# A two-layer attention trunk: norm weights applied at the evacuation of the turned blocks, value projections token by token

## The chip, the cores and the metric

One NeuronCore of one Trainium2 chip runs the kernel. The metric is the device time of one execution in microseconds (us).

## The reference

Two layers work on x of 512 tokens by 1024 channels: `x <- x + RMSNorm(Mixer(RMSNorm(x, norm_pre[i])), norm_post[i])`. Layer 0 mixes with sparse attention of three branches (compressed, selected, window; 16 heads in 4 groups), layer 1 with differential attention (8 heads). What the change touches is the start of each:

```python
u = rmsnorm(x, norm_pre[i])          # x * rsqrt(mean(x*x) + EPS) * g
q, kc, vc, ks, vs, kw, vw, gate, z = jnp.split(u @ w_in, points, axis=-1)   # layer 0
gate = sigmoid(gate)
q, k, v, z = jnp.split(u @ w_in, 4, axis=-1)                               # layer 1
```

All is float32.

## The kernel before, in words

**Products.** Every operand of a projection is cut in two parts of type float32r: hi, a rounded copy, and lo, the rest. A projection is then three products (hi x hi, lo x hi, hi x lo). Activations are turned so that channels lie on partitions: eight blocks of 128 channels for each of four token tiles of 128 tokens. The turned u is kept as `bigA` (hi) and `bigB` (lo) in layer 0, `bigF` and `bigE` in layer 1; `bigD` and `bigC` hold the normed x before it is turned.

**Norm.** `prenorm` (L355) takes one token tile: two Squares with sums on ScalarE (L361), a few 128x1 instructions on VectorE for the root (L335 to L352), and two 128x512 passes that write x * r * g (L373; g is a row of norm weights spread over all partitions, tiles `P`, loaded at L298 as two transfers of 256 KB). In layer 1 (`early`) GpSimd multiplies with g beforehand (L364) and VectorE scales with two pointer scalars (L369). `turn` transposes four blocks into one PSUM bank `T` (L380), and ScalarE and VectorE evacuate the bank in one instruction each: hi (L100, 128x512) and lo (L105, 128x512).

**Weights.** `Stream` loads weight pieces on the SP queue (L126) and splits them into whi and wlo. Who splits is set by tables: the first letter names the engine of the hi (A ScalarE, P GpSimd), the second that of the lo (D VectorE, P GpSimd). Without an entry GpSimd does both (L165, L167). Each split lets the load of the second next piece follow on the SP queue.

**Start.** The jobs `vs` and `vw` (value projections, 256 and 304 columns; 48 of the 304 are the gate) come first, then the compressed keys and values `kc0, kc1, vc0, vc1` (L198, 24 matmuls of 128x512 each, evacuated by `evac_cmp` with two ScalarE and two VectorE copies, L399 and L400, from the two `mm` banks). The value jobs use L218; `vw` runs cut by cut over all tokens, two tokens in a bank. `turn_small` (L711, L714) comes between kc1 and vc0. The gate's Tanh is taken per token in `evac_v` (L432), and one VectorE instruction scales the gate (L780, 128x192, two immediate numbers). Seven matmuls on zeros (L306) run before the first data.

**Between the layers.** `o1` is the second half of layer 0's output projection (L467). While it ends, VectorE and GpSimd norm the tokens of layer 1. `dv0` and `dv1` are the first value projections there; the order of token tiles is written out in `SEQ` (a and b are steps of dv0 and dv1 with the token's number, p is a `turn`), TensorE keeping exactly that order. dv0 keeps two tokens in each of two `S` banks; ScalarE evacuates it at L571. VectorE makes the lo of dv1's first piece (L160, tile `wx`), GpSimd its hi.

## Time and profile before

| | us |
|---|---|
| median of 3 runs | 666.04 |
| lowest, highest | 665.90, 666.87 |
| profiled execution: its own time | 669.65 |
| profiled execution: span | 667.8 |
| TensorE busy | 638.7 (96%) |
| VectorE busy | 427.7 (64%) |
| GpSimd busy | 401.6 (60%) |
| ScalarE busy | 338.9 (51%) |

The chain of work that ended last is 78% TensorE, 14% VectorE, 3% ScalarE, 2% DMA, 2% issue. The mean granted clock of the profiled execution is 0.986 of full. The span is the stretch from the first to the last instruction of the trace; the execution's own time is 1.85 longer, and the profiled execution took 3.61 longer than the median of the timed runs. In the 40 slices of the page TensorE is at 90% or more nearly everywhere; the first two slices (0 to 33 us) show 6 and 8 tenths.

### The profile page before, as it was taken

The page shows a single profiled execution, that of the slowest core. Times are in us where ns is not written, and L with a number is a line of the kernel's source. Part 1 is how long each engine was busy: PE and PEld are TensorE (multiplying, and loading weights), DVE is VectorE, ACT ScalarE, POOL GpSimd, SP SyncE. Part 2 cuts the span into 40 slices and gives each one's busy share as a digit, 9 for nine tenths or more (in the row PEclk, how much of TensorE's full clock was granted, in tenths as well). Part 3 has the DMA queues.
Part 4 walks back from the last instruction along what each step waited for, and adds up shares of the span by engine and source line. Part 5 has one row for each costly group of instructions (what it writes and reads, how often), then busy time and mean ns, then how long its engine had stood idle before and what let it go on. Part 6 is the DMA issues. An engine that isn't in the chain of part 4 may idle for free.

```text
span 667.8 us, 11248 instructions
## 1 busy us (share of the span) xinstructions
PE 638.7 (96%) x3773; PEld 558.1 (84%) x3773; DVE 427.7 (64%) x1188; ACT 338.9 (51%) x904; POOL 401.6 (60%) x675
## 2 busy tenths in 40 slices
PE   6899999999999999999999899999999998989996
PEld 5897887888788788888887799888988887879785
DVE  4736245678878878969878800146559658777635
ACT  5311134676667567868563311235464564658431
POOL 4766757868677597668586458948565564413200
PEclk8899999999999999999999999999999998989999
DMA  7546333212122111200852222423223131115302
GB/s 250 151 127 140 107 103 94 64 33 64 32 64 62 35 31 51 62 17 34 301 179 95 95 64 67 124 63 111 73 72 105 47 97 41 62 63 191 126 19 107
DMA packets 68989, 60.52 MB, mean 91 GB/s; under 512 B 3628, under 2 KB 60868, under 8 KB 68932
## 3 DMA queue, kind: packets, MB, share of 16 engines
q1 hardware_dynamic: 68212, 57.45, 29.2%
q10 hardware_dynamic: 720, 2.36, 0.9%
q8 instruction: 30, 0.49, 0.3%
q14 instruction: 27, 0.22, 0.1%
HBM read 55.04 MB, written 4.76 MB: 90 GB/s over the span
## 4 chain that ended last, share of the span: by engine, by line
PE 78%; DVE 14%; ACT 3%; issue 2%; DMA 2%; POOL 0%; SPq 0%; DVEq 0%; ACTq 0%; POOLq 0%
PE mm L198 30%; PE mm L218 11%; PE mm L467 6%; PE T L856 5%; PE av L870 5%; PE S L801 4%; PE S L218 4%; PE S L800 4%; PE S L467 3%; PE av L1166 2%; DVE stk L105 2%; DVE gate L780 2%; PE T L721 1%; PE T L1156 1%; DMA wraw<-in_nsa_w_in_dram 1%
## 5 line engine op out<-in xcount | busy, mean ns | idle before, releaser
L167 POOL TENSOR_TENSOR wlo<-wraw,whi 128x256 fp32r<-128x256 f32 (+2 forms) x247 | 184.0, 772 | 26.9 <-ACT whi L163 26.9
L165 POOL TENSOR_SCALAR whi<-wraw 128x256 fp32r<-128x256 f32 (+1 forms) x240 | 96.2, 426 | 112.7 <-PE mm L198 51.9
L794 ACT ACTIVATE P<-P,st 128x512 f32<-128x512 f32 (+3 forms) x192 | 107.5, 560 | 91.8 <-DVE st L792 91.0
L850 POOL TENSOR_SCALAR P<-P,st,gate 128x512 f32<-128x512 f32 (+3 forms) x128 | 80.1, 636 | 27.1 <-DVE st L847 24.1
L792 DVE CUSTOM_DVE_ANT_0 P<-S,BT 128x128 f32<-128x128 f32 (+2 forms) x144 | 59.7, 419 | 31.2 <-PE S L801 29.0
L198 PE MATMUL mm<-bigA,whi 128*128 128x512 f32 x192 | 77.4, 403 | 1.3 <-DVE bigC L400 1.2
L198 PE MATMUL mm<-bigA,wlo 128*128 128x512 f32 x192 | 75.3, 392 | 0.0
L198 PE MATMUL mm<-bigB,whi 128*128 128x512 f32 x192 | 75.3, 392 | 0.0
L105 DVE TENSOR_TENSOR PT<-T,PT 128x512 fp32r<-128x512 f32 x84 | 56.9, 685 | 8.3 <-ACT PT L100 6.4
L870 PE MATMUL av<-PT,bigE 128*128 128x512 f32 x160 | 56.4, 417 | 1.2 <-DVE bigF L878 0.9
L100 ACT ACTIVATE stk<-mm 64x512 fp32r<-64x512 f32 x64 | 37.9, 592 | 33.2 <-PE mm L198 19.0
L218 PE MATMUL mm<-whi,bigF 128*128 128x256 f32 x176 | 51.4, 293 | 1.7 <-DVE stk L105 1.7
L856 PE MATMUL T<-ident,P 128*128 128x128 f32 x320 | 51.8, 272 | 0.0
L198 PE MATMUL mm<-bigF,whi 128*128 128x512 f32 x128 | 51.7, 404 | 0.0
L100 ACT ACTIVATE PT<-T 128x512 fp32r<-128x512 f32 x84 | 48.6, 592 | 6.0 <-PE T L856 3.9
L198 PE MATMUL mm<-bigF,wlo 128*128 128x512 f32 x128 | 51.3, 401 | 0.0
L856 PEld LDWEIGHTS T<-ident,P 128*128 128x128 f32 x320 | 40.9, 140 | 12.3 <-issue 0.4
L198 PE MATMUL mm<-bigE,whi 128*128 128x512 f32 x128 | 51.1, 399 | 0.0
L218 PE MATMUL mm<-whi,bigE 128*128 128x256 f32 x176 | 50.6, 289 | 0.0
L218 PE MATMUL mm<-wlo,bigF 128*128 128x256 f32 x176 | 50.6, 288 | 0.0
L421 DVE SCALAR_TENSOR_TENSOR stk<-mm,stk 64x512 fp32r<-64x512 f32 x32 | 22.1, 690 | 44.2 <-ACT stk L100 43.4
L198 PEld LDWEIGHTS mm<-bigB,whi 128*128 128x128 f32 x192 | 36.1, 188 | 8.2
(288 smaller groups left out, 1663.4 us busy)
## 6 DMA issues: line engine op xcount, KB each, us to landing
wraw<-in_diff_w_in_dram SPq DMA_DIRECT2D x31, 512.0 KB, 4.0
wraw<-in_nsa_w_in_dram SPq DMA_DIRECT2D x26, 512.0 KB, 3.8
BT<-rd SPq DMA_DIRECT2D x32, 128.0 KB, 3.6
wraw<-in_diff_w_out_dram SPq DMA_DIRECT2D x5, 512.0 KB, 4.0
bigF<-in_x_dram SPq DMA_DIRECT2D x4, 512.0 KB, 9.7
wraw<-in_nsa_w_out_dram SPq DMA_DIRECT2D x4, 512.0 KB, 3.5
bigD<-in_x_dram SPq DMA_DIRECT2D x4, 512.0 KB, 4.7
x1d<-bigD ACTq DMA_DIRECT2D x4, 512.0 KB, 5.2
```

Source lines behind the costliest of these rows:

```text
L100: return nc.scalar.activation(dst, src, AF.Copy, scale=scale)
L105: nc.vector.tensor_tensor(dst, src, h.bitcast(F32), op=OP.subtract)
L165: nc.gpsimd.tensor_scalar(h[:, a:b], v, 1.0, 0.0, op0=OP.mult, op1=OP.add)
L167: e.tensor_tensor(l[:, a:b], v, h[:, a:b].bitcast(F32), op=OP.subtract)
L198: T["mm"] = nc.tensor.matmul(p[:, a:b], wt[:, k, :], u[:, k, a:b], start=(k == 0 and j == 0), stop=(k == KD - 1 and j == 2)).ins
L218: nc.tensor.matmul(acc[t], u[:, k0 + k, t * 128:(t + 1) * 128], wt[:, k, :], start=(ci == 0 and k == 0 and j == 0 and t % per == 0), stop= ...
L467: nc.tensor.matmul(p, U[u][:, k, t * 128:(t + 1) * 128], wt[wi], start=start and j == 0, stop=stop and j == 2, skip_group_check=True)
L792: nc.vector.tensor_tensor_reduce(out=o, in0=i0, in1=b, op0=OP.add, op1=OP.min, scale=-1.0, scalar=BIG, accum_out=nm)
L794: nc.scalar.activation(pt[:, :n], pt[:, :n], AF.Exp, bias=nm, scale=-1.0, accum_out=den)
L850: NORM(nc, i, br, qb).tensor_scalar(self.P[i][:, :n], self.P[i][:, :n], st[:, 8 + i:9 + i], gate[:, NT - 1 - qb, c:c + 1], op0=OP.mult, op ...
L856: T["tmark"] = nc.tensor.transpose(p[:, j * 128:(j + 1) * 128], self.P[j][:, kb * 128:(kb + 1) * 128], ident).ins
L870: nc.tensor.matmul(av, T["V"][:, br, kb, g, :], p, start=(br == 0 and kb == 0 and j == 0), stop=(br == 1 and kb == qb and j == 1))
```

## The change

- **Start.** x's first tile comes in two halves; the norm weights come as 8x128 on the ScalarE queue (4 KB), are turned by TensorE into `gT` (one channel per partition) and copied out (L317). The prenorm of layer 0 then only scales (L385, two pointer scalars), and the norm weight enters at the evacuation: eight ScalarE copies with a scale and eight VectorE instructions (L399), each 128x128, for every token tile, in place of two and two of 128x512. Tiles 1 to 3 take one Square of 1024. Twelve warm-up matmuls in place of seven.
- **Value projections.** `vs` and `vw` run token by token in the order of `SEQ0` (s and w with the token's number, a and b six and two of its eight steps, p a `turn`), each token in a bank of its own. Five pieces are split ahead, vw's hi by ScalarE and lo by GpSimd or VectorE; kc0's and kc1's pieces are split when vw is done.
- **Gate.** It is copied per token, and one Tanh follows for all four.
- **Between the layers.** p1 moves from inside o1 to the head of `SEQ`; dv0 takes one bank per token (S, T, S, S); dv1's first piece is split by ScalarE (hi) and GpSimd (lo).

```diff
-WARM = 7
+WARM = 12
-PRE1 = 29
...
-NS = 4
+NS = 5
...
-SPD = ('PD',)*4
-SEQ = 'a0 a1 p2 b0 b1 a2 p3 b2 a3 b3'.split()
+SPD = ('AP',)*4
+SEQ0 = 's0a p1 s0b s1 w0 w1a p2 w1b s2 w2a p3 w2b w3 s3'.split()
+SEQ = 'p1 a0 a1 p2 b0 b1 a2 p3 b2 a3 b3'.split()
-SPX = ('AP',) * 4
-SPN = 2
-SP0 = ('AP',)*4
-SP1 = ('AD','AD','PP','PP')
+SP0 = (('AP', 'AD', 'AP', 'AP'), ('AD', 'AP', 'AD', 'AP'), ('AP', 'AP', 'AD'), ('AP', 'AP', 'AD'), ('AP', 'AD'))
...
-            bs = [bank(b) for b in banks]
-            per = 4 // len(bs)
-            acc = [bs[t // per][:, (t % per) * n:(t % per) * n + n] for t in range(NT)]
+            if by_token:
+                per, acc = 1, [None] * NT
+            else:
+                bs = [bank(b) for b in banks]
+                per = 4 // len(bs)
+                acc = [bs[t // per][:, (t % per) * n:(t % per) * n + n] for t in range(NT)]
...
             if by_token:
                 for ci in range(len(cuts)):
                     cut[ci] = ws.cut.pop(i + ci)
                 for t in range(NT):
+                    acc[t] = bank(banks[t * len(banks) // NT])[:, :n]
                     for ci in range(len(cuts)):
                         yield from part(ci, t)
                     evac(t, acc[t])
-                for _ in cuts:
-                    if i:
-                        ws.split()
+                for _ in range(len(cuts) if nsplit is None else nsplit):
+                    ws.split()
...
-    load_x(0)
-    gpre = [ptile() for _ in range(2)]
     for i in range(2):
-        nc.sync.dma_start(gpre[i], drows(npre, i * 512, [[0, 128], [1, 512]]))
+        nc.sync.dma_start(xt[:, 0, i * 512:i * 512 + 512], drows(x, i * 512, [[D, 128], [1, 512]]))
+    g8 = work.tile([8, 128], F32, name="g8", tag="P", bufs=NP)
+    gload = nc.scalar.dma_start(g8, drows(npre, 0, [[128, 8], [1, 128]])).ins
...
+    with tc.manual_schedule(engines={mybir.EngineType.PE}):
+        warm(WARM - 7)
+        p = bank("T")
+        nc.tensor.transpose(p[:, 0:8], g8, ident[0:8, 0:8])
+        warm(7)
+    T0["g"] = nc.vector.tensor_copy(gT, p[:, 0:8]).ins
...
+        whole = t and not early
         ss = [small(1, tag="ss") for _ in range(2)]
-        with tc.issue_after(T0["a"]) if "a" in T0 else ExitStack():
-            for c, s in zip(halves, ss):
+        with tc.issue_after(T0["a"]) if early and "a" in T0 else ExitStack():
+            for c, s in ((slice(0, D), ss[1]),) if whole else zip(halves, ss):
                 nc.scalar.activation(pttile(F32) if early else xn[:, c], src[:, c], AF.Square, accum_out=s)
         if early:
             for c, g in zip(halves, grow):
-                nc.gpsimd.tensor_tensor(xn[:, c], src[:, c], g, op=OP.mult)
-        m0 = part_sum(ss[0])
+                T["xm"] = nc.gpsimd.tensor_tensor(xn[:, c], src[:, c], g, op=OP.mult).ins
+        m0 = epst if whole else part_sum(ss[0])
         if early:
             r, q = row_rstd(m0, ss[1], split=True)
             for c in halves:
                 nc.vector.tensor_scalar(xn[:, c], xn[:, c], r, q, op0=OP.mult, op1=OP.mult)
         else:
-            r = row_rstd(m0, ss[1])
-            for c, g in zip(halves, grow):
-                nc.vector.scalar_tensor_tensor(xn[:, c], src[:, c], r, g, op0=OP.mult, op1=OP.mult)
+            r, q = row_rstd(m0, ss[1], split=True)
+            with tc.issue_after(T0["l"]) if "l" in T0 else ExitStack():
+                for c in halves:
+                    T0["s"] = nc.vector.tensor_scalar(xn[:, c], src[:, c], r, q, op0=OP.mult, op1=OP.mult).ins
...
-                x = hi(uh[:, i * 4:i * 4 + 4, cs], pv).ins
-                T0["h"] = x
-                if t == 0:
-                    T0["a"] = x
-                lo(ul[:, i * 4:i * 4 + 4, cs], pv, uh[:, i * 4:i * 4 + 4, cs])
+                if not early:
+                    for j in range(4):
+                        k = i * 4 + j
+                        T0["h"] = hi(uh[:, k, cs], pv[:, j], gT[:, k:k + 1]).ins
+                        T0["l"] = nc.vector.scalar_tensor_tensor(ul[:, k, cs], pv[:, j], gT[:, k:k + 1],
+                                                                 uh[:, k, cs].bitcast(F32), op0=OP.mult,
+                                                                 op1=OP.subtract).ins
+                    continue
+                T0["h"] = hi(uh[:, i * 4:i * 4 + 4, cs], pv).ins
+                T0["l"] = lo(ul[:, i * 4:i * 4 + 4, cs], pv, uh[:, i * 4:i * 4 + 4, cs]).ins
...
-                nc.scalar.activation(T["gate"][:, NT - 1 - t, :], p[:, 256:304], AF.Tanh, scale=0.5)
+                nc.scalar.activation(T["gate"][:, NT - 1 - t, :], p[:, 256:304], AF.Copy)
...
-    tjob("vs", w_in, NSA_IN, 1792, 256, evac_v(0), ("S", "S", "mm", "mm"), by_token=True)
-    tjob("vw", w_in, NSA_IN, 2304, 304, evac_v(1), ("mm", "mm", "S", "S"), cuts=((0, 3), (3, 3), (6, 2)))
+    tjob("vs", w_in, NSA_IN, 1792, 256, evac_v(0), ("S", "S", "S", "S"), by_token=True, nsplit=0)
+    tjob("vw", w_in, NSA_IN, 2304, 304, evac_v(1), ("mm", "S", "S", "mm"), cuts=((0, 3), (3, 3), (6, 2)), by_token=True,
+         nsplit=2)
...
-             by_token=n == 0)
+        tjob(f"dv{n}", dw_in, DIFF_IN, 2048 + n * 256, 256, evac_dv(n),
+             (("S", "T", "S", "S"), ("mm", "mm"), ("S", "S"), ("mm", "mm"))[n], by_token=n == 0)
...
+    with tc.issue_after(T0["g"]):
+        xnorm(0)
+    root0 = T0["a"]
+    with tc.issue_after(T0["s"]):
         ws.split()
+    with tc.manual_schedule(engines={mybir.EngineType.PE}):
+        turns[0]()
+    with tc.issue_after(T0["h"]):
+        ws.split()
+    with tc.issue_after(T0["s"]), tc.issue_after(root0):
+        xnorm(1)
...
-    for t in range(NT):
-        prenorm(t, xt[:, t], xn[:, t], gpre, U["h"], U["l"], False)()
-        for _ in range(8):
-            run.step()
-
-    with tc.issue_after(T0["h"]):
-        nc.scalar.activation(small(1, tag="rstd"), epst, AF.Tanh)
+    with tc.manual_schedule(engines={mybir.EngineType.PE}):
+        gens = [jobs[index[n]].run(jobs[index[n]].first) for n in ("vs", "vw")]
+        for w in SEQ0:
+            t = int(w[1])
+            if w[0] == "p":
+                turns[t]()
+            else:
+                for _ in range({"": 8, "a": 6, "b": 2}[w[2:]]):
+                    next(gens["sw".index(w[0])])
+            if w == "p1":
+                with tc.issue_after(T0["h"]):
+                    for _ in range(2, NS):
+                        ws.split()
+                with tc.issue_after(T0["l"]), tc.issue_after(T0["h"]):
+                    xnorm(2)
+                    xnorm(3)
+        for g in gens[::-1]:
+            for _ in g:
+                pass
+    run.i = 2
+    run.done += jobs[0].cost + jobs[1].cost
+    nc.scalar.activation(gate, gate, AF.Tanh, scale=0.5)
...
-        while run.i <= index["o1"]:
-            run.step()
-            if run.done - T.setdefault("o1b", run.done) > PRE1 * 640:
-                if ("pre", 1) in T:
-                    T.pop(("pre", 1))()
+        run.upto("o1")
         T["dv"] = slot("A", [128, NT, D])
         U["h"], U["l"] = U1["h"], U1["l"]
         ws.split()
         gens = [jobs[index[n]].run(jobs[index[n]].first) for n in ("dv0", "dv1")]
-        for w in SEQ:
-            if w[0] == "p":
-                T["pre", int(w[1])]()
-            else:
-                for _ in range({"a": 8, "b": 4}[w[0]]):
-                    next(gens["ab".index(w[0])], None)
-        for g in gens:
-            for _ in g:
-                pass
+        with tc.issue_after(T["xm"]):
+            for w in SEQ:
+                if w[0] == "p":
+                    T["pre", int(w[1])]()
+                else:
+                    for _ in range({"a": 8, "b": 4}[w[0]]):
+                        next(gens["ab".index(w[0])], None)
+            for g in gens:
+                for _ in g:
+                    pass
```

VectorE at the start, before (bigA, bigB are hi and lo of the turned u, T a bank of transposes):

```order
L373 SCALAR_TENSOR_TENSOR bigD_166<-bigF_72,rstd_173,P_74 128x512
L373 SCALAR_TENSOR_TENSOR bigD_166<-bigF_72,rstd_173,P_75 128x512
L105 TENSOR_TENSOR bigB_165<-T_184,bigA_164 128x4x128
L160 TENSOR_TENSOR bigC_115<-wraw_110,bigC_115 128x256 x2
L105 TENSOR_TENSOR bigB_165<-T_191,bigA_164 128x4x128
```

and in the changed kernel:

```order
L385 TENSOR_SCALAR bigD_133<-bigF_72,rstd_140,rs3_142 128x512 x2
L356 SCALAR_TENSOR_TENSOR rs1_204<-ss_201,epst_81 128x1
L157 TENSOR_TENSOR bigC_150<-wraw_125,bigC_150 128x256
L357 RECIPROCAL rstd_203<-rstd_203 128x1
L358 SCALAR_TENSOR_TENSOR rs3_205<-rstd_203,rs1_204 128x1
L359 TENSOR_SCALAR rs3_205<-rs3_205 128x1
L399 SCALAR_TENSOR_TENSOR bigB_132<-T_163,gT_88,bigA_131 128x128
L399 SCALAR_TENSOR_TENSOR bigB_132<-T_176,gT_88,bigA_131 128x128
```

The two 128x512 lo passes of token tile 0 became eight of 128x128 that alternate between its two banks (two of them shown), and the scaling no longer reads the norm weights.

VectorE where the gate is scaled, before (L400 is the evacuation of kc0):

```order
L105 TENSOR_TENSOR bigE_162<-S_435,bigE_162 128x4x64
L105 TENSOR_TENSOR bigE_162<-S_436,bigE_162 128x4x64
L780 TENSOR_SCALAR gate_163<-gate_163 128x192
L400 COPY bigC_424<-mm_577 64x8x32
L634 MEMSET rt_161 16x128
L400 COPY bigC_424<-mm_577 64x8x32
```

and in the changed kernel (L826 is the line of L780, L417 that of L400):

```order
L102 TENSOR_TENSOR bigE_219<-mm_518,bigE_219 128x4x64
L826 TENSOR_SCALAR gate_220<-gate_220 128x192
L102 TENSOR_TENSOR bigE_219<-S_545,bigE_219 128x4x64
L417 COPY bigC_626<-mm_633 64x8x32 x2
L668 MEMSET rt_218 16x128
```

The gate's instruction now stands ahead of the last lo of vs as well as ahead of kc0's evacuation.

The SP queue from kc0's weights on, before (479 and 527 are the pieces of kc1 and vc0):

```order
L126 DMA wraw_154<-in_nsa_w_in_dram 128x8x128
L621 DMA tab_156<-in_rel_bias_table_dram 32x16
...
L688 DMA sub8_414<-in_diff_subln_dram 8x128
L126 DMA wraw_479<-in_nsa_w_in_dram 128x8x128
L126 DMA wraw_527<-in_nsa_w_in_dram 128x8x128
L126 DMA wraw_575<-in_nsa_w_in_dram 128x8x128
```

and in the changed kernel (294, 583, 595 and 668 are those of kc1, vc0, vc1 and ks0):

```order
L123 DMA wraw_294<-in_nsa_w_in_dram 128x8x128
L123 DMA wraw_583<-in_nsa_w_in_dram 128x8x128
L123 DMA wraw_595<-in_nsa_w_in_dram 128x8x128
L724 DMA bigF_601<-in_nsa_cmp_w1_k_dram 128x16x128
L726 DMA pe0_603<-in_nsa_cmp_pe_k_dram 32x64
...
L734 DMA sub8_616<-in_diff_subln_dram 8x128
L123 DMA wraw_668<-in_nsa_w_in_dram 128x8x128
```

The loads for the compression (its weights, `pe`, `sub8`) stand behind vc1's piece now, and ahead of ks0's.

TensorE between the layers, before (L380 is the turn of token tile 1; L218 to bank S is dv0):

```order
L467 MATMUL S<-wx,bigA 128x512 x2
L467 MATMUL S<-wx,bigB 128x512
L380 MATMUL T<-ident,bigC 128x128 x8
L467 MATMUL S<-wx,bigA 128x512 x2
L467 MATMUL S<-wx,bigB 128x512
L218 MATMUL S<-whi,bigF 128x256
L218 MATMUL S<-wlo,bigF 128x256
L218 MATMUL S<-whi,bigE 128x256
```

and in the changed kernel (L484 is the line of L467, L392 that of L380):

```order
L484 MATMUL S<-wx,bigA 128x512 x2
L484 MATMUL S<-wx,bigB 128x512
L484 MATMUL S<-wx,bigA 128x512 x2
L484 MATMUL S<-wx,bigB 128x512
L392 MATMUL T<-ident,bigC 128x128 x8
L218 MATMUL S<-whi,bigF 128x256
L218 MATMUL S<-wlo,bigF 128x256
L218 MATMUL S<-whi,bigE 128x256
```

The turn of tile 1 moved behind the last three matmuls of o1, directly ahead of dv0.

## Rows read from the trace of the kernel before

**Rows 1.** Waits by releaser, TensorE, 0 to 60 us: total, times, longest.

```profile
PE T L380 <- DVE bigD L373: 3.0, 4, 1.4
```

**Rows 2.** Timeline, ScalarE and TensorE, 3 to 60 us: start, duration, operation, idle before.

```profile
9.48 1.33 ACT L100 ACTIVATE bigC<-wraw 128x256 fp32r<-128x256 f32 x4 [3.78 <-DMA wraw<-in_nsa_w_in_dram]
...
11.34 0.80 PE L218 MATMUL S<-bigC,bigA 128*128 128x256 f32 x2 [1.85 <-ACT bigA L100]
...
20.31 0.38 PE L218 MATMUL S<-bigC,bigB 128*128 128x256 f32 x1 [1.84 <-DVE bigB L105]
...
45.37 0.30 PE L218 MATMUL S<-whi,bigB 128*128 128x304 f32 x1
45.51 0.39 PE L198 MATMUL mm<-bigA,whi 128*128 128x512 f32 x1
...
59.01 0.47 PE L198 MATMUL mm<-bigA,whi 128*128 128x512 f32 x1 [1.19 <-DVE bigC L400]
```

**Rows 3.** Groups by form, ScalarE and VectorE, 0 to 62 us: busy, mean ns, idle.

```profile
L100 ACT ACTIVATE bigA<-T 128x512 fp32r<-128x512 f32 x8 | 4.7, 593 | 8.0 <-PE T L380 8.0
...
L373 DVE SCALAR_TENSOR_TENSOR bigD<-bigF,rstd,P 128x512 f32<-128x512 f32 x8 | 7.1, 909 | 0.8 <-DMA P<-in_norm_pre_dram 0.6
L105 DVE TENSOR_TENSOR bigB<-T,bigA 128x512 fp32r<-128x512 f32 x8 | 5.4, 681 | 4.9 <-ACT bigA L100 4.9
...
L105 DVE TENSOR_TENSOR bigE<-mm,bigE 128x256 fp32r<-128x256 f32 x4 | 1.7, 424 | 11.9 <-ACT bigE L100 11.9
```

**Rows 4.** Timeline, issues of the SP queue, 0 to 45 us.

```profile
13.03 12.28 SPq L126 DMA_DIRECT2D wraw<-in_nsa_w_in_dram  x4
...
26.86 0.85 SPq L678 DMA_DIRECT2D bigF<-in_nsa_cmp_w_k_dram  x1
...
37.43 7.59 SPq L126 DMA_DIRECT2D wraw<-in_nsa_w_in_dram  x2
```

**Rows 5.** Windows: busy time by engine, granted clock (PEclk), DMA share, GB/s.

```profile
11.16:14.57 3.41, 3.23 (x13) 3.01 (x14) 3.14 (x7) 2.97 (x10) 3.41 (x6) 0.50 0.62 226
21.39:24.80 3.41, 3.41 (x19) 3.41 (x18) 3.31 (x7) 1.19 (x2) 3.41 (x5) 0.50 0.31 91
...
371.00:374.00 3.00, 0.56 (x5) 0.42 (x4) 3.00 (x6) 0.95 (x5) 1.01 (x1) 1.00 0.85 307
```

**Rows 6.** Timeline, VectorE, 44 to 61 us.

```profile
46.82 10.71 DVE L780 TENSOR_SCALAR gate<-gate 128x192 f32<-128x192 f32 x1 [0.28 <-ACT gate L432]
57.57 0.42 DVE L400 COPY bigC<-mm 64x256 f32<-64x256 f32 x1
```

**Rows 7.** Timeline, GpSimd, 38 to 62 us.

```profile
40.32 1.51 POOL L165 TENSOR_SCALAR whi<-wraw 128x256 fp32r<-128x256 f32 x4 [4.63 <-PE mm L218]
41.80 2.82 POOL L167 TENSOR_TENSOR wlo<-wraw,whi 128x256 fp32r<-128x256 f32 x4
...
57.63 1.51 POOL L165 TENSOR_SCALAR whi<-wraw 128x256 fp32r<-128x256 f32 x4 [0.21 <-PE mm L198]
```

**Rows 8.** Timeline, TensorE and VectorE, 364 to 385 us.

```profile
366.31 1.25 PE L380 MATMUL T<-ident,bigC 128*128 128x128 f32 x8 [0.97 <-DVE bigC L369]
...
373.58 0.39 PE L218 MATMUL S<-whi,bigF 128*128 128x256 f32 x1 [2.44 <-ACT bigA L571]
...
383.79 1.04 PE L380 MATMUL T<-ident,bigC 128*128 128x128 f32 x8
...
367.09 2.35 DVE L1052 SCALAR_TENSOR_TENSOR bigD<-bigC,rstd,bigD 128x512 f32<-128x512 f32 x2
369.36 3.26 DVE L160 TENSOR_TENSOR wx<-P,wx 128x256 fp32r<-128x256 f32 x3
372.55 0.14 DVE L335 TENSOR_SCALAR m<-ss 128x1 f32<-128x1 f32 x1
```

**Rows 9.** Groups by form, VectorE and GpSimd, 360 to 386 us.

```profile
L369 DVE TENSOR_SCALAR bigC<-bigC,rstd,rs 128x512 f32<-128x512 f32 x6 | 3.4, 605 | 0.1
...
L364 POOL TENSOR_TENSOR bigC<-bigD,P 128x512 f32<-128x512 f32 x6 | 9.1, 1539 | 8.9 <-DVE bigD L1052 8.9
```

40 lines of the change are left out of this document (22 added, 18 removed).

## The prediction

> **What bounds it now.** I read the shares of busy time first: TensorE is at 96%, so only its idle time and its slow stretches can be won back, some 28 us. The waits of TensorE by window say where these lie. In the start its transposes wait 3.0 us for VectorE's normed x [rows 1], the first projection waits 1.85 for ScalarE's hi and one later 1.84 for VectorE's lo [rows 2]. Then kc0, kc1 and the rest run dense, but for 1.19 us ahead of vc0 at 59.01 [rows 2]. The next stretch with waits that the change touches is the step to layer 1: 0.97 and 2.44 us [rows 8]. The clock view comes last: after two pauses of TensorE in the start (1.85 and 1.84) 3.41 us each ran at a granted clock of 0.50, the lower level of 1.2 GHz, while after the 2.44 us at 371.1 it stayed at 1.00 [rows 5]. So a pause may cost 3.41 / 2 = 1.7 us more than itself, and need not.
>
> I forecast by milestones: kc0's first matmul (45.51 now), vc0's first (59.01, thus 13.5 behind), and the last turn of layer 1 (383.79) [rows 2, 8]. What follows each is unchanged and dense, so a shift carries through to the end.
>
> **Start, up to kc0: about +0.8 (gain).** Removed: two 256 KB broadcasts ahead of the first weights on the SP queue. The first weights landed at 9.45, when ScalarE's hi began [rows 2]; of the 1.5 MB up to and with them (x's first tile, the broadcasts, the first piece) a third goes, so I take some 7 us. The scaling is L385 in place of L373: 0.909 us on average [rows 3], against 0.605 for the same form with two pointer scalars [rows 9]. Added: five warm-up matmuls and a transpose, which hold TensorE until about 8.1 and delay nothing, since the first normed tile is ready at about 7.6. The evacuation is the dear part: two hi of 0.593 and two lo of 0.681 become eight and eight of 128x128. From 0.681 for 512 and 0.424 for 256 columns [rows 3] VectorE needs 0.30 for 128 columns, ScalarE by the same ratio 0.26. Both engines alternate between two banks, hi of one beside lo of the other, so a pair of blocks takes 0.6 to 0.7 and a tile 2.6 to 2.9 us, about what the two chains of hi and lo took one after the other (2 x 1.27). It costs ScalarE 8 x 0.26 - 2 x 0.59 = 0.9 us a tile, and VectorE 1.0, less what the scaling saves.
>
> Walked through: tile 0 is evacuated from 9.0 to 11.9; vs of token 0 ends at 15.9, paced by its evacuation and by w1's split; tile 1 is evacuated by 18.8, and vs of token 1 ends at 19.0. Then vw's pieces bind. ScalarE, which makes their hi now, is free of tile 1 only at 18.5; the first piece's lo frees the load buffer at 20.6, the third piece is loaded by 23.5, split by 25.0, and TensorE, which has reached it at 22.5, idles 2.4 us. Token 0 of vw ends at 25.5. What remains is three tokens of vw, 24 matmuls at 0.14 from start to start [rows 2], 10.1 us; two of vs at 0.12 (the same by columns), 5.8; two turns, 1.7; together 17.6, and 0.9 for evacuations that come late. kc0 then starts at 44.0, 1.5 earlier. If the idle 2.4 us bring one slow stretch, 1.7 of it is lost: -0.2. The rows have pauses of that length with and without a fall, so I take the middle, +0.8, and keep both ends.
>
> **Gate, up to vc0: -0.95.** L780 needs a fraction of a microsecond by size, but took 10.71, from 46.82 to 57.53 [rows 6]. GpSimd ran split after split, without a pause, from 40.32 to 57.42, then waited 0.21 for TensorE [rows 7]; VectorE's instruction ended there. kc0's evacuation was queued behind it (57.57), and vc0 needs that bank: 59.01 - 57.57 = 1.44 later. In the changed kernel L826 is the same form, and reaches the head of VectorE 0.3 us before kc0 starts. GpSimd starts kc0's split when the first cut of vw's last token is done, 5.1 us before kc0 (P), and has four pieces of 1.51 + 2.82 = 4.3 and two memsets of 0.5 in a row: until P + 17.8. The fifth piece, ks0's, can't be there: its load stands behind the small loads of the compression, which took from 26.86 to 37.43 to issue [rows 4], and these behind vc1's piece, issued when kc1's split is done (P + 8.9). So it lands at about P + 23, GpSimd pauses at P + 17.8, 12.7 after kc0's start; the last lo of vs (0.42) and the 1.44 follow: vc0 starts 14.5 after kc0, against 13.5. Without a hold it would be 11.75: the 13.5 less the 1.19 and less the half microsecond of `turn_small`, which moves into vc0. The loads that moved are used inside vc0 and vc1, and land before that; no wait of TensorE comes from them.
>
> Against this stands a rule of the Trainium skill (SBUF — State Buffer, "Who interferes with whom"): VectorE's two-port modes and GpSimd exclude each other, and whoever issues first has the shared pair for its whole instruction. By it the gate would wait for one GpSimd instruction, under 0.8 us, and vc0 would start at 11.75: +1.75 in place of -0.95. The row of 10.71 us, over more than twenty instructions of GpSimd, speaks against that reading, and I go by the row.
>
> **Step to layer 1: +2.1.** dv0's second token waits 2.44 us for L571, the evacuation of the first, with which it shares a bank. ScalarE is late with it because the root of a norm is queued ahead of it, and that waits for L335 on VectorE (372.55), which stands behind three lo of dv1 at 1.09 each (369.36, 3.26 us) [rows 8]. With a bank per token the second token needs only tile 1's evacuation; with L160 gone to GpSimd, VectorE is free for that from 369.4, when L1052 ends. Two lo of 0.68 bring 370.9; the turn itself, now behind o1, starts at 366.3 to 367.3 without a wait, and dv0 ends its first token at about 370.4. So 0.5 us is left of the 2.44, up to 2.0 if VectorE takes another norm first. The 0.97 goes, since o1's last matmuls fill it; 0.4 ahead of the turn of tile 3 stays. The price is four lo on GpSimd, beside L364 there (1.54 each [rows 9]); they end some 4 us before dv1 reads them, if GpSimd takes them ahead of the next norm, and cost up to 1 us if not. Gain 1 to 3, nearest to 2.1.
>
> **Sum.** 0.8 - 0.95 + 2.1 = 1.95: the profiled execution of 669.65 would be 667.7, and the median, 3.61 below it, 664.1 from 666.04.
>
> **Rivals.** (1) *The gate gets in early.* Two pieces are due close on GpSimd's heels: each is issued when a buffer comes free, lands 3.6 to 3.8 us later, and is wanted after 4.3. If one is half a microsecond late, GpSimd pauses at P + 8.9 or P + 13.2, the gate passes, and vc0 has no wait: 0.8 + 1.75 + 2.1 = 4.65, thus 661.4. For it: w1_k now loads right behind vc1's piece. Against it: the same distance held in the kernel before, without a gap [rows 7]. The rule of the Trainium skill quoted above would bring the same time. (2) *The clock falls at vc0.* TensorE's pause there grows from 1.19 to 2.75 us. If it brings a stretch at 0.50, as two of 1.85 did, and one of 2.44 did not [rows 5], 1.7 more is lost: 665.8. (3) *The gate is held longer: slower.* If ks0's piece has landed by P + 17.8, GpSimd goes on without a pause, VectorE is held for another 4.3 us, and vc0 starts 18.8 after kc0: 0.8 - 5.25 + 2.1 = -2.35, thus 668.4. The small loads decide: they took 10.6 us to issue, and would have to take under about 5. Some of that time was waiting for landings, so it may be. (4) That the change does not do what it says: the step to layer 1 loses its 2.1 if VectorE or GpSimd there is simply late with the next thing; then 666.2, inside the range.
>
> **Chances.** Forecast 0.36, with its parts' bounds 662 to 666; rival 1 0.28; rival 2, and 4 with it, 0.20; rival 3 0.16. A measurement of this kernel tells 0.2%, or 1.33 us, from no change. Faster by more: 0.26 of the forecast, all of rival 1, 0.02 of rival 2: 0.56. Within: 0.08, 0.15 and 0.02 of rival 3: 0.25. Slower: 0.19. The range leaves out rival 3 and the last of rival 1 (with the start's +1.5 and the step's 3 it would be 659.8): 660.4 to 667.2.
>
> **What would show it.** In the changed profile: kc0's first matmul at 43.8 to 45.7; a wait of TensorE for L417 of 2 to 3 us ahead of vc0, and L826 at some 13 us, ending where GpSimd pauses. In rival 1 L826 is short, or ends at an earlier pause, and that wait is gone; in rival 3 it is over 16 us. PEclk shows 0.50 after vw's first token or after vc0's pause, or not. The waits for L571 should be gone from the step to layer 1, and the last turn should come 2 us earlier against kc0. I am wrong if kc0 starts later than 46, if TensorE waits for GpSimd's lo in dv1, or if anything behind the last turn moves by more than 1 us.

## The result, and the profile after

The changed kernel takes 669.64 us (median of 7 runs, 668.44 to 674.43) against 665.90 for the kernel before (7 runs, 663.07 to 666.87): a ratio of 1.0073, 95% interval 1.0045 to 1.0102 (the ratio is taken from all runs, the slowest of the changed kernel included, and is larger than that of the medians, 1.0056). It is **slower by 3.7 us** by the medians, where 664.1 was forecast and the range ended at 667.2. The profiled execution took 674.43, its span 672.6: the longest of its seven, 4.8 above the median, and 4.8 above the span of before.

Four milestones of the two traces show where the time lies. A shift between two of them is what the stretch between them cost. The first is kc0's second matmul and not its first, because in the changed kernel the first (48.43) stands ahead of the last token of vs:

```profile
45.74 0.39 PE L198 MATMUL mm<-bigA,wlo 128*128 128x512 f32 x1
```

```profile
48.43 0.39 PE L195 MATMUL mm<-bigA,whi 128*128 128x512 f32 x1
...
51.94 0.40 PE L195 MATMUL mm<-bigA,wlo 128*128 128x512 f32 x1
```

| start, us | before | after | difference |
|---|---|---|---|
| kc0's second matmul | 45.74 | 51.94 | +6.20 |
| turn of tile 0 of layer 1 | 359.53 | 365.88 | +6.35 |
| turn of tile 3 of layer 1 | 383.79 | 387.88 | +4.09 |
| end of the span | 667.8 | 672.6 | +4.8 |

So in these two traces the start lost 6.2 us, the step between the layers gave 2.3 back, and the rest is even to a microsecond. On the page (busy tenths and granted clock in 40 slices) TensorE is busier in the first two slices, 7 and 9 tenths against 6 and 8 before, and its clock is lower in the second, 7 against 8:

```profile
PE   7999999999999999999999999999999998989996
PEclk8799999999999999999999999999999998989999
```

Four stretches of the start, by windows (busy time of TensorE, weight loads, VectorE, ScalarE and GpSimd; then granted clock, DMA share, GB/s):

```profile
12.70:22.70 10.00, 8.40 (x38) 7.88 (x37) 6.47 (x17) 5.00 (x17) 1.60 (x2) 0.50 0.35 99
22.70:29.70 7.00, 5.74 (x36) 4.64 (x35) 3.22 (x10) 5.89 (x16) 4.55 (x5) 0.99 0.36 93
29.70:33.00 3.30, 3.29 (x13) 3.30 (x14) 2.75 (x9) 0.59 (x2) 0.00 (x0) 0.50 0.79 217
33.00:51.70 18.70, 18.29 (x129) 16.88 (x128) 6.89 (x21) 8.61 (x25) 5.38 (x12) 1.00 0.01 2
```

The clock is at 0.50, its level of 1.2 GHz, for about 13.6 us in place of 6.8 [rows 5]. TensorE's waits there (0 to 66 us; total, times, longest):

```profile
PE S L218 <- DVE bigC L157: 1.6, 1, 1.6
PE S L218 <- ACT bigA L97: 1.3, 2, 1.0
...
PE mm L218 <- ACT whi L97: 0.6, 1, 0.6
PE mm L218 <- POOL wlo L157: 0.5, 1, 0.5
```

The 3.0 us for the normed x [rows 1] are gone, and the two of 1.8 [rows 2] became smaller ones; vc0's wait of 1.19 for the gate is gone as well. By the waits alone the start should have gained. It did not: TensorE's work between 12.7 and 22.7 us, at half clock, counts as busy and not as a wait, and what it waits for comes later at each step. The timeline shows the first two token tiles on ScalarE and VectorE (start, duration, operation, idle before):

```profile
9.29 1.33 ACT L97 ACTIVATE bigC<-wraw 128x256 fp32r<-128x256 f32 x4 [0.53 <-DMA wraw<-in_nsa_w_in_dram]
...
10.72 0.60 ACT L97 ACTIVATE bigA<-T,gT 128x128 fp32r<-128x128 f32 x2
11.94 0.62 ACT L97 ACTIVATE bigA<-T,gT 128x128 fp32r<-128x128 f32 x2 [0.62 <-DVE bigB L399]
12.73 0.62 ACT L97 ACTIVATE bigA<-T,gT 128x128 fp32r<-128x128 f32 x2 [0.16 <-DVE bigB L399]
13.52 0.63 ACT L97 ACTIVATE bigA<-T,gT 128x128 fp32r<-128x128 f32 x2 [0.16 <-DVE bigB L399]
14.04 1.32 ACT L97 ACTIVATE bigC<-wraw 128x256 fp32r<-128x256 f32 x4
```

```profile
11.50 0.15 DVE L359 TENSOR_SCALAR rs<-rs 128x1 f32<-128x1 f32 x1
11.57 0.60 DVE L399 SCALAR_TENSOR_TENSOR bigB<-T,gT,bigA 128x128 fp32r<-128x128 f32 x2
12.34 0.61 DVE L399 SCALAR_TENSOR_TENSOR bigB<-T,gT,bigA 128x128 fp32r<-128x128 f32 x2 [0.18 <-ACT bigA L97]
...
13.92 0.61 DVE L399 SCALAR_TENSOR_TENSOR bigB<-T,gT,bigA 128x128 fp32r<-128x128 f32 x2 [0.18 <-ACT bigA L97]
14.45 1.40 DVE L385 TENSOR_SCALAR bigD<-bigF,rstd,rs 128x512 f32<-128x512 f32 x2
15.77 1.27 DVE L157 TENSOR_TENSOR bigC<-wraw,bigC 128x256 fp32r<-128x256 f32 x2
```

ScalarE writes two hi, then waits for the lo of the two before; VectorE writes two lo, then waits for the next hi. A pair of blocks (two hi and two lo) comes every 0.79 us (11.94, 12.73, 13.52). The first lo stands behind the root of tile 1's norm (L357 to L359), which ends at 11.65, and ScalarE waits 0.62 for it. Tile 0 takes 0.62 + 4 x 0.79 = 3.8 us, from 10.72 to 14.53. All that is queued behind on the two engines comes late with it: the hi of vs's second weight piece (14.04; the w1 whose split the prediction names), the scaling of tile 1 (14.45), that piece's lo (15.77), and at 16.76 TensorE has waited 1.60 for that lo. Tile 1, by its first hi and its last lo, takes 4.3 us:

```profile
19.09 0.37 ACT L97 ACTIVATE bigA<-T,gT 128x128 fp32r<-128x128 f32 x1 [3.73 <-PE T L392]
...
23.02 0.35 DVE L399 SCALAR_TENSOR_TENSOR bigB<-T,gT,bigA 128x128 fp32r<-128x128 f32 x1 [0.44 <-ACT bigA L97]
```

### The profile page after: what moved, and what is told of

The parts are those of the page before. It is cut to its first block, busy times and chain, and to the rows that moved or that the text cites. A ratio compares the mean times of both kernels' runs of the same rounds, so it can differ in the third digit from the quotient of the medians.

```text
span 672.6 us, 11304 instructions
## 1 busy us (share of the span) xinstructions
PE 649.2 (97%) x3784; PEld 563.4 (84%) x3784; DVE 414.9 (62%) x1206; ACT 349.4 (52%) x936; POOL 393.1 (58%) x661
## 4 chain that ended last, share of the span: by engine, by line
PE 79%; DVE 12%; ACT 3%; DMA 2%; issue 2%; POOL 1%; SPq 0%; DVEq 0%; ACTq 0%; POOLq 0%
PE mm L195 31%; PE mm L218 10%; PE mm L484 6%; PE T L902 5%; PE av L916 5%; PE S L218 5%; PE S L847 4%; PE S L846 4%; PE S L484 3%; DVE stk L102 2%; PE av L1209 2%; DMA wraw<-in_nsa_w_in_dram 2%; PE T L767 1%; PE T L1199 1%; DVE P L838 1%
## 5 line engine op out<-in xcount | busy, mean ns | idle before, releaser
L164 POOL TENSOR_TENSOR wlo<-wraw,whi 128x256 fp32r<-128x256 f32 (+1 forms) x239 | 176.2, 766 | 26.7 <-ACT whi L160 26.7
L162 POOL TENSOR_SCALAR whi<-wraw 128x256 fp32r<-128x256 f32 x232 | 91.0, 419 | 102.3 <-PE mm L195 44.1
L218 PE MATMUL mm<-whi,bigF 128*128 128x256 f32 x176 | 51.8, 296 | 1.7 <-DVE stk L102 1.7
L218 PE MATMUL mm<-whi,bigE 128*128 128x256 f32 x176 | 50.8, 290 | 0.0
L218 PE MATMUL mm<-wlo,bigF 128*128 128x256 f32 x176 | 50.8, 289 | 0.0
```

The source lines that it names most:

```text
L162: nc.gpsimd.tensor_scalar(h[:, a:b], v, 1.0, 0.0, op0=OP.mult, op1=OP.add)
L164: e.tensor_tensor(l[:, a:b], v, h[:, a:b].bitcast(F32), op=OP.subtract)
L218: T["tm"] = nc.tensor.matmul(acc[t], u[:, k0 + k, t * 128:(t + 1) * 128], wt[:, k, :], start=(ci == 0 and k == 0 and j == 0 and t % per == 0),
```

## The experiments

For each experiment the table gives the measured median, the ratio to the kernel before on the same chip with its interval, and from its trace the time from the first matmul of vs to kc0's second, and how long in the start the clock stood at 0.50.

| | median us | ratio (95%) | vs to kc0 | at 0.50 |
|---|---|---|---|---|
| before | 665.90 | 1 | 34.4 | 6.8 |
| after | 669.64 | 1.0073 (1.0045 to 1.0102) | 40.8 | 13.6 |
| e1 gate and step | 662.92 | 0.9953 (0.9937 to 0.9969) | 32.3 | 6.8 |
| e2 step | 663.37 | 0.9954 (0.9936 to 0.9972) | 32.3 | 6.8 |
| e3 x later | 671.62 | 1.0071 (1.0051 to 1.0092) | 38.3 | 3.4 |
| e4 fillers | 672.17 | 1.0080 (1.0058 to 1.0102) | 38.8 | 0 |
| e5 old norm | 663.21 | 0.9969 (0.9952 to 0.9986) | 32.4 | 3.4 |
| e6 GpSimd split | 669.27 | 1.0051 (1.0030 to 1.0071) | 38.7 | 6.8 |
| e7 both | 667.06 | 1.0002 (0.9986 to 1.0017) | 34.7 | 0 |
| e10 blocks | 670.83 | 1.0066 (1.0050 to 1.0081) | 39.3 | 6.8 |
| e11 x between | 666.37 | 0.9992 (0.9976 to 1.0009) | 32.0 | 3.4 |
| e13 two pairs | 662.47 | 0.9949 (0.9932 to 0.9966) | 31.8 | 0 |
| e14 four pairs | 663.79 | 0.9969 (0.9955 to 0.9983) | 34.3 | 3.4 |
| e15 eight pairs | 669.78 | 1.0048 (1.0028 to 1.0068) | 38.2 | 6.8 |
| e16 hi, then lo | 666.81 | 1.0009 (0.9994 to 1.0024) | 34.3 | 0 |

**e2, e1: the step between the layers alone; with the gate.** e2 is the kernel before with the new `SPD`, `SEQ` and banks of dv0. e1 adds the gate's part:

```diff
-                nc.scalar.activation(T["gate"][:, NT - 1 - t, :], p[:, 256:304], AF.Tanh, scale=0.5)
+                nc.scalar.activation(T["gate"][:, NT - 1 - t, :], p[:, 256:304], AF.Copy)
...
+    nc.scalar.activation(gate, gate, AF.Tanh, scale=0.5)
```

> The kernel before with the step to layer 1 alone (turn of tile 1 behind o1, one bank per token in dv0, dv1's first piece split by ScalarE and GpSimd). Theory 1: first to last turn of layer 1 takes 22.0 us as in the changed kernel against 24.3 before, and the time is 2.0 to 2.5 us below the kernel before. Theory 2 (moved wait): the stretch shrinks, but the time stays within 0.5 us. The gate's instruction is as in the kernel before, held for about 10.7 us.

> The start of the kernel before (norm weights by broadcast, evacuation of 128x512, vs and vw in the old order) with the two other parts of the change: the gate by one Tanh after four copies, and the step to layer 1. Theory 1 (the whole loss of the change lies in its start): this is faster than the kernel before, by the 2.3 us that the step to layer 1 gained between its first and its last turn, and by 1.2 more if the gate's instruction is no longer held: 662.5 to 663.7 against 666. Theory 2 (the step to layer 1 only moves a wait, which comes back later): no change, 665.5 to 666.5. Theory 3 (the gate's instruction went through in the changed kernel because of one Tanh instead of four): here it takes about 0.5 us too; if it is the moment at which it comes that decides, it is held for some 10 us again.

Both are faster than before, by 3.2 and 3.6 us against the 666.54 of the kernel before on their chip. From the turn of tile 0 to that of tile 3 it took 22.04 and 22.03 us, against 24.26: the step is worth 2.2, and what is left of their gain is no more than the start varies by itself: with the same order of instructions, vs to kc0 took 32.3 us in the traces of e1, e2, e9 and e12, and 34.4 in that of before. The gate's part, 1.2 us in the traces (below), does not show in the times: 0.9953 with it, 0.9954 without. So the start is what made the whole change slow.

**e3: x's second tile loaded behind the weights; e4: TensorE kept busy in its pauses.**

```diff
-    load_x(1)
     ws.load()
     ws.load()
+    load_x(1)
```

```diff
+        fill(4)
         for w in SEQ0:
...
+                    fill({("s0a", 4): 6, ("w0", 6): 6}.get((w, k), 0))
```

`fill` issues so many matmuls of 128x256 on zeros into a bank that nothing reads.

> The changed kernel with the load of x's second tile moved behind the first two weight pieces on the SP queue. Theory A (the late weights are the root: their hi stands ahead of tile 0's evacuation on ScalarE, and the lo of the second piece ahead of vs): the first weights land about 1.3 us sooner than 9.3, tile 0's evacuation starts at 9.5 in place of 10.7, and kc0's second matmul (51.94 in the changed kernel) comes 1.5 to 2.5 us earlier. Theory B (the low clock is the loss): under 0.7 us, unless the slow stretch of 10 us gets shorter. Theory C (the evacuation in blocks of 128x128 is the loss): under 1 us, with the same 0.79 us per pair of blocks.

> The changed kernel with 16 extra matmuls on zeros where TensorE waits in the start: four ahead of vs, six ahead of the first matmul on the second weight piece, six ahead of vw's third piece. Theory B (TensorE's pauses bring the low clock, and this is the loss): the granted clock stays at 1.00 from 12.7 to 33, and kc0's second matmul comes 3 to 5 us earlier than 51.94. Theories A and C: the clock may stay high, but evacuation and splits set the pace, and kc0 comes at most 2 us earlier.

Neither helps. In e3 the first weights' hi starts at 6.86 in place of 9.29, but tile 0's evacuation still starts at 10.64, since tile 1's Square stands ahead of it on ScalarE and x's second tile is what comes late now:

```profile
9.58 1.06 ACT L372 ACTIVATE bigD<-bigF 128x1024 f32<-128x1024 f32 x1 [1.21 <-DMA bigF<-in_x_dram]
```

In e4 the clock never fell in the start:

```profile
10.00:52.00 42.00, 40.91 (x258) 35.59 (x257) 23.78 (x70) 23.91 (x67) 13.49 (x24) 1.00 0.24 70
```

and vs to kc0 still took 38.8 us. Its fillers are work themselves (six took 2.75), so e4 shows a start that is slow without any fall, and does not measure the clock's share.

**e5: the old norm; e6, e7: vw split by GpSimd.** e5 puts the two broadcasts, L373's form and the evacuation in two hi and two lo of 128x512 back into the changed kernel, and x's second tile behind the first two weight pieces, where the kernel before loads it (the change had moved it ahead of them); it leaves all else. e6 is the changed kernel with all eight parts of vw's pieces split by GpSimd, ahead of tile 1's evacuation; e7 is both.

```diff
-                        T0["h"] = hi(uh[:, k, cs], pv[:, j], gT[:, k:k + 1]).ins
...
+                T0["h"] = hi(uh[:, i * 4:i * 4 + 4, cs], pv).ins
+                T0["l"] = lo(ul[:, i * 4:i * 4 + 4, cs], pv, uh[:, i * 4:i * 4 + 4, cs]).ins
```

> The changed kernel with the norm of the kernel before: weights by two broadcasts, loads in the old order, one hi and one lo of 128x512 per bank. Token order, banks and who splits vw's pieces stay as in the change. Theory C (the evacuation in 128x128 blocks is the loss): from the first matmul of vs to kc0's second it takes 40.8 us in the changed kernel and 32.3 in the run with the old start; here at most 35, and the time is that of that run, 663 to 664. Theory D (the order of vw's work is the loss: its pieces are split by ScalarE, only after tile 1 is evacuated, some 6 us later than GpSimd did it): 38 to 40 us, and 667 to 670.

> The changed kernel with vw's three pieces split by GpSimd alone (hi and lo), ahead of and beside the evacuation of tile 1, as in the kernel before. Theory D: the first piece is split from about 17 instead of 22.9, the third by about 27, the waits of 0.6 and 0.5 us ahead of it go with the slow stretch after them, and kc0's second matmul comes 2.5 to 4 us earlier than in the changed kernel. Theory C: under 1.5 us.

> Both: the old norm and evacuation, and vw's pieces split by GpSimd; left of the change in the start are the fixed order of tokens, a bank per token, twelve warm-ups. If C and D together are the loss: 32 to 33.5 us from vs to kc0, and 662.5 to 664. If the fixed order itself (TensorE may not pass a waiting token) costs: over 35 us, and above 665.5.

e5 turns the result round: 663.21, kc0 at 43.42. The token order, the banks, the gate and the step are sound, and the loss is in the part that applies the norm weights or in the order of the loads that came with it (e13, below, has the loads of the change and is as fast as e5). GpSimd is no way out: e6 cannot be told from the changed kernel, and beside the old norm it costs 3.9 us by the medians (667.06), where TensorE then waits 2.2 us for GpSimd's lo and 1.7 for tile 0's hi (0.4 in e5).

**e11: x's second tile between the two weight pieces; e10: blocks of 128x128 without the scale.** Both on e5:

```diff
     ws.load()
+    load_x(1)
     ws.load()
-    load_x(1)
```

```diff
+                if not early:
+                    for j in range(4):
+                        k = i * 4 + j
+                        T0["h"] = hi(uh[:, k, cs], pv[:, j]).ins
+                        T0["l"] = lo(ul[:, k, cs], pv[:, j], uh[:, k, cs]).ins
+                    continue
```

> The run with the old norm, with x's second tile loaded between the first two weight pieces. There TensorE waited 1.7 us for the normed tile 1, and a slow stretch of 3.4 us stood around that wait. Theory B'' (that tile is late by its load): the wait goes, and 1 to 2.5 us with it: 661 to 662.2. Otherwise (the second weight piece is then late in its place): 662.7 to 664.

> The run with the old norm again, but with the evacuation in sixteen instructions of 128x128 per token tile, without a scale: what is left of the norm weights' move is the number of instructions alone. Theory C1 (the number is the loss): a tile's evacuation takes 3.6 to 4.3 us again in place of 1.9, vs to kc0 38 to 41 us in place of 32.4, and the time is 668 to 671. Theory C2 (the scale operand or the load and turn of the norm weights is the loss): 32 to 34 us, and 663 to 664.5.

e11 loses 3.2 us to e5 by the medians, 1.5 by the ratios, whose intervals overlap. In its trace tile 1's Square (10.93) came ahead of tile 0's evacuation (11.98) on ScalarE, and vs's first matmul waited 2.9 for tile 0's hi: the order of the loads sets what ScalarE does first. e10 is as slow as the changed kernel, 670.83, without any scale operand. But in it ScalarE took the Square of tile 1, which waited for its load, between two blocks of tile 0, and TensorE waited 1.87 there. So e10 does not tell the number of instructions from that accident, and four more runs change the evacuation alone.

**e13, e14, e15: two, four and eight pairs of a hi and a lo for a tile, without the norm weights; e16: the changed kernel, the four hi of a bank ahead of its four lo.** In e13 to e15 n is 4, 2 and 1:

```diff
-                    for j in range(4):
+                    for j in range(0, 4, n):
                         k = i * 4 + j
-                        T0["h"] = hi(uh[:, k, cs], pv[:, j], gT[:, k:k + 1]).ins
...
+                        T0["h"] = hi(uh[:, k:k + n, cs], pv[:, j:j + n]).ins
+                        T0["l"] = lo(ul[:, k:k + n, cs], pv[:, j:j + n], uh[:, k:k + n, cs]).ins
```

> The changed kernel in all but the evacuation of the turned blocks in the start: two hi and two lo of 128x512 for a token tile again; the norm weights are left out. Theory A (the number of instructions of the evacuation cost the start its 6 us): a tile in about 1.9 us from the first hi to the last lo, as with the old norm; 32 to 34 us from the first projection matmul to kc0, median 662.5 to 664.5. Theory B (the scale operand costs it): the same, so that this run tells A and B together from theory C. Theory C (the order of the loads without the broadcasts, or the token order with this norm): 37 us or more, median 667 or more.

> As the run before, with four hi and four lo of 128x256 for a token tile (norm weights left out). Theory A: between two and eight: a tile in 2.2 to 2.9 us, 33 to 36 us from the first projection matmul to kc0, median 663.5 to 667. Theory B: no scale operand, so as with two pairs, 662.5 to 664.5.

> As the two before, with eight hi and eight lo of 128x128 for a token tile, without the scale operand (norm weights left out); the order of every engine is that of the changed kernel within a row or two, so the difference to the changed kernel is the scale operand, and to the run with two pairs the number of instructions. Theory A: a tile in 2.9 to 3.5 us, 36 to 39.5 us to kc0, median 666 to 670. Theory B: within 1 us of the run with two pairs, 662.5 to 665.

> The changed kernel with the norm weights, but in each bank the four hi first and then the four lo, in place of hi and lo by turns. If the hand-over between the two engines at every pair of blocks (0.16 to 0.18 us each) is what makes the eight pairs dear: ScalarE is through with a tile's eight hi after some 2.5 us in place of 3.4, kc0 1 to 3 us earlier, median 667 to 669. If the instructions' own time is: a tile is still 3.5 us or more, and the median 669 to 671.

662.47, 663.79, 669.78: the number of instructions brings the whole loss, and with the scale (669.64) it is no more. The order of the two engines is not quite the same in the three. In e14, e15 and the changed kernel the evacuation of vs's first token stands between the blocks of tile 1 (in e15 ScalarE waits for it),

```profile
20.52 0.38 ACT L97 ACTIVATE bigE<-S 128x256 fp32r<-128x256 f32 x1 [0.83 <-PE S L218]
```

and in e13 and e16 behind them. From e14 to e15, with the same order of ScalarE and VectorE up to kc0, it is 6.0 of the 7.3 us (3.6 of 4.2 among the runs at a granted clock of 0.991), so this is not what the loss hangs on. Groups by form, 0 to 60 us, ScalarE and VectorE (busy, mean ns, idle before) of the changed kernel:

```profile
L97 ACT ACTIVATE bigA<-T,gT 128x128 fp32r<-128x128 f32 x32 | 10.5, 364 | 11.6 <-PE T L392 9.0 <-DVE bigB L399 2.3
...
L399 DVE SCALAR_TENSOR_TENSOR bigB<-T,gT,bigA 128x128 fp32r<-128x128 f32 x32 | 10.2, 347 | 9.9 <-ACT bigA L97 9.7
```

of e15:

```profile
L97 ACT ACTIVATE bigA<-T 128x128 fp32r<-128x128 f32 x32 | 7.7, 276 | 10.9 <-PE T L392 9.0 <-DVE bigB L102 1.9
...
L102 DVE TENSOR_TENSOR bigB<-T,bigA 128x128 fp32r<-128x128 f32 x32 | 8.1, 286 | 8.4 <-ACT bigA L97 6.8
```

and of e13:

```profile
L97 ACT ACTIVATE bigA<-T 128x512 fp32r<-128x512 f32 x8 | 4.3, 592 | 7.1 <-PE T L392 7.1
...
L102 DVE TENSOR_TENSOR bigB<-T,bigA 128x512 fp32r<-128x512 f32 x8 | 5.1, 685 | 6.8 <-ACT bigA L97 6.8
```

A quarter of the columns takes 276 of 592 ns and 286 of 685, and the wait of ScalarE for VectorE (2.3 and 1.9 in all) is not there with two pairs. The scale operand lengthens one hi to 364 and one lo to 347; by the medians that decides nothing, by the ratios (1.0073 and 1.0048, with intervals that overlap) it may cost some 1.7 us. The Trainium skill (VectorE: DVE Perf Modes, the section on the TRN2 errata) says of VectorE's and ScalarE's instructions that read SBUF that each pays a fixed extra latency, so that one large tile pays it once and many small ones each time, and advises 512 elements or more. The blocks here come out of a PSUM bank (the lo reads hi from SBUF beside it), and these rows agree in kind: the time falls much less than the columns.

e16 keeps all 16 instructions of a tile and the scale, and only the order differs:

```profile
10.55 2.15 ACT L97 ACTIVATE bigA<-T,gT 128x128 fp32r<-128x128 f32 x8
12.55 1.37 ACT L97 ACTIVATE bigC<-wraw 128x256 fp32r<-128x256 f32 x4
16.65 2.18 ACT L97 ACTIVATE bigA<-T,gT 128x128 fp32r<-128x128 f32 x8 [2.74 <-PE T L392]
```

```profile
11.70 2.16 DVE L401 SCALAR_TENSOR_TENSOR bigB<-T,gT,bigA 128x128 fp32r<-128x128 f32 x8 [0.21 <-ACT bigA L97]
```

A tile still takes 3.3 us (10.55 to 13.86), but ScalarE runs its eight hi in 2.15 without a wait and is at vs's second weight piece at 12.55 in place of 14.04; tile 1 is turned at 16.01 in place of 18.00. The median falls by 2.8 us to 666.81, by 1.9 among the runs at a clock of 0.988 (667.7 and 669.6). Not all of it need be the turn-taking of the two engines: vs's first token has moved behind tile 1's blocks as well, and from kc0's second matmul to layer 1's first turn e13 to e16 take 312.6 us, the changed kernel 313.9, a difference behind the start that no run here explains. So the turn-taking is some 2 to 3 us of the loss at most. The rest stays with eight pairs: e16, in the same order of ScalarE as e13 and like it without a fall of the clock in the start, is 4.3 us slower, where a tile takes 3.3 us in place of 2.1.

**Is it the clock?** In the changed kernel's trace the clock costs up to 6.8 / 2 = 3.4 us more than in that of before. That is a good part of the 6.2 that the start lost there. But each timed run has its mean granted clock, and among runs of equal clock the order of the kernels stays. At 0.991: e5 663.2 (4 runs), e13 663.4 (4), e14 664.0 (6), before 665.4 (7), e16 666.6 (2), e15 667.6 (2), after 668.4 (1). At 0.988: before 665.0 (10 runs), e16 667.7 (5), after 669.6 (3). And in the traces of e4 and e16 the start had no fall at all and still took 38.8 and 34.3 us, against 31.8 in e13, which had none either. The falls add to the loss; they do not make it.

**e8: a filled, written order for the start of e1.** TensorE's order of vs and the turns is written out, with six zero matmuls behind the first turn:

```diff
+        for w in "p0 f s0a p1 s0b s1a p2 s1b s2a p3 s2b s3a s3b".split():
```

> The old start with the gate and the step to layer 1 of the change (the first run), and TensorE's order written out: each turn ahead of the last three steps of the token before it, and six matmuls on zeros between the first turn and vs. Theory B' (what is left to win in the old start is the slow stretch of 6.8 us and the waits of 2.3 for an evacuation): the slow stretch goes or halves, vs to kc0 takes 28.5 to 30.5 us against 32.3, and the time is 660 to 662. Otherwise (the splits set the pace): as the first run, 662.5 to 663.5.

666.23 (12 runs; 0.9997, interval 0.9980 to 1.0015), 3.3 above e1, kc0 at 46.53, two stretches at 0.50 all the same: a miss.

**e9, e12: what holds the gate.** e9 is e1 with four Tanh in place of the one, e12 the same with two Copies of 48 columns ahead of the last.

```diff
-    nc.scalar.activation(gate, gate, AF.Tanh, scale=0.5)
+    for t in range(NT):
+        nc.scalar.activation(gate[:, NT - 1 - t, :], gate[:, NT - 1 - t, :], AF.Tanh, scale=0.5)
```

> The first run, with the gate's Tanh in four instructions, one per token, behind the copies, in place of one for all. In ten traces so far the gate's instruction on VectorE was held until GpSimd paused (10.7 us) in the two with four Tanhs, and passed at GpSimd's next boundary between two instructions in the eight with one. Theory W (the four writers decide it): it is held for some 10 us. Theory M (the moment decides: both times it was held it had come 0.04 us behind the start of one of GpSimd's subtractions): it passes in under 0.8 us, unless it comes within 0.1 us of such a start again.

> The run with four late Tanhs, with two copies of 48 columns in place put ahead of the last Tanh, so that the gate's instruction reaches VectorE some 0.45 us later, after about 1.0 us without work there. In 13 traces it was held in the three with four Tanhs, which are also the three where VectorE had been idle for 0.55 us or less (in the others 0.67 or more). Theory W (four writers decide): held for some 10 us again. Theory I (the length of VectorE's idle time decides, or something that goes with it): it passes in under 0.8 us.

One run each: 663.93 and 664.30 us. The gate on VectorE in the changed kernel, with GpSimd beside it:

```profile
52.07 0.52 DVE L826 TENSOR_SCALAR gate<-gate 128x192 f32<-128x192 f32 x1 [1.95 <-ACT gate L717]
...
50.98 1.51 POOL L162 TENSOR_SCALAR whi<-wraw 128x256 fp32r<-128x256 f32 x4
52.45 1.44 POOL L164 TENSOR_TENSOR wlo<-wraw,whi 128x256 fp32r<-128x256 f32 x2
```

of e2, e9 and e12, in this order:

```profile
44.80 10.72 DVE L784 TENSOR_SCALAR gate<-gate 128x192 f32<-128x192 f32 x1 [0.28 <-ACT gate L436]
```

```profile
44.91 10.44 DVE L786 TENSOR_SCALAR gate<-gate 128x192 f32<-128x192 f32 x1 [0.55 <-ACT gate L785]
```

```profile
45.50 9.89 DVE L789 TENSOR_SCALAR gate<-gate 128x192 f32<-128x192 f32 x1 [1.10 <-ACT gate L788]
```

With one Tanh VectorE gets in where one GpSimd instruction ends and the next begins (52.07 + 0.52 against 52.45), though GpSimd makes no pause. So it was in all 14 traces with one Tanh (0.26 to 0.61 us), and in all four with four Tanh (before, e2, e9, e12) it was held some 10 us. VectorE's idle time before it does not tell the two apart: e12 was held after 1.10 us, e1 got in after 0.67. Why the writers of its operand should decide stays open. The Trainium skill's rule that the prediction quotes (SBUF — State Buffer, "Who interferes with whom") fits the 14 and not the four.

## Why the prediction was wrong

- **The evacuation of the turned blocks, the step that failed.** The prediction took eight and eight blocks to need about the time of the two and two before. The working put a pair of blocks at "0.6 to 0.7", a tile at "2.6 to 2.9 us, about what the two chains of hi and lo took one after the other (2 x 1.27)". A pair takes 0.64 without the scale (e15: hi at 11.70, 12.34, 12.97), as worked out, and 0.79 with it: hi goes from 276 to 364 ns, lo from 286 to 347, which no row of before showed. To four pairs come 0.62 for VectorE's roots, which stand ahead of the first lo: 3.8 us for tile 0, 4.3 for tile 1 (19.09 to 23.37). And the measure it was held against was wrong, which weighs more, since e15 has the 0.64 and is as slow: the two chains overlap, hi of one bank beside lo of the other, so the old way takes 1.9 us (10.35 to 12.25 in e5):

```profile
10.35 1.06 ACT L97 ACTIVATE bigA<-T 128x512 fp32r<-128x512 f32 x2
...
10.96 1.29 DVE L102 TENSOR_TENSOR bigB<-T,bigA 128x512 fp32r<-128x512 f32 x2 [0.27 <-ACT bigA L97]
```

The term stood at nothing for the path and at 0.9 for ScalarE; it is some 2 us a tile on the path of the first two tiles, and what waits behind them.
- **What follows from it was walked right, in part by luck.** Tile 0 was to be evacuated from 9.0 to 11.9. ScalarE had the hi of the first weights ahead of it, so it began at 10.72, and at 10.35 in e5 and 10.63 in e13. With two pairs a tile takes 1.9 to 2.1 us in place of 2.9 and ends at 12.25 and 12.76: the late start and the short evacuation nearly cancel. From there the walk holds to a microsecond or so in these two runs: tile 1 evacuated by 18.8 forecast, 18.42 and 17.93; vw's third piece loaded at 23.5 forecast, its hi at 22.95 and 22.40; kc0 at 44.0 forecast, its second matmul at 43.42 and 43.03. In the changed kernel tile 0 ends at 14.53, tile 1 at 23.37, the third piece's hi comes at 28.29 and kc0's second matmul at 51.94: 2.6 us behind the forecast, then 4.6, 4.8 and 7.9. TensorE ran 10.2 us of this stretch in one piece at half clock; how the growth divides between that and engines and load buffers that come free later is not shown.
- **The first weights.** Taken at some 7 us, they landed at 9.3. The change also loads x's second tile ahead of them, which the section on the change does not say and the prediction missed; with that load behind them (e3) their hi starts at 6.86. It gains nothing by itself, since tile 0's evacuation then waits behind x's second tile.
- **The clock** was taken as a stretch more or none, at 1.7 us. In the profiled execution it was two stretches' worth more, 3.4 us, one of them 10 us long in one piece.
- **The gate.** The mechanism fell: forecast was a hold of 13 us and 0.95 lost, measured 0.52 us and no wait of vc0; rival 1's outcome came true by another way, since GpSimd made no pause. By the second compression (33.91 us after kc0's second matmul, 34.41 before) half a microsecond is won, and by layer 1's first turn nothing is left (313.94 against 313.79). In e1 against e2 the same edit brings 1.2 us up to the first compression (17.59 against 18.80).
- **The step to layer 1** was right. Forecast +2.1, measured 24.26 - 22.00 = 2.26; e2 and e1, 2.2. TensorE's waits between 350 and 395 us:

```profile
PE T L218 <- DVE bigE L102: 1.0, 1, 1.0
PE T L392 <- DVE rstd L362: 0.3, 1, 0.3
```

The 2.44 and 0.97 [rows 8] are gone, the second token waits 1.0 for its lo (0.5 to 2.0 forecast), and no wait for GpSimd's lo came.

With the measured terms the sum is -6.2 (start) - 0.15 (to layer 1) + 2.26 (step) - 0.7 (behind the last turn) = -4.8, the difference of the spans. The chance given to slower was 0.19, 0.14 of it for a longer hold of the gate and the rest from the upper ends of the forecast and of rivals 2 and 4; no rival named the evacuation, though the text called it "the dear part". Two readings of the prediction were slightly off and move no sum: TensorE's idle time was 29.1 us (667.8 - 638.7) and not some 28, and the first fall of the clock, at 11.16 [rows 5], began inside the pause of 1.85 us that ended at 11.34 [rows 2], not after it.
